# A hybrid decoder trunk: gate and up with seven block products for eight in two k pairs of eight, and each FFN in two parts

## The chip, the core and the metric

The kernel runs on one core of one Trainium2 chip. The metric is the device time of one execution in microseconds; the median over several runs counts. Engines are named as in the profile: PE is TensorE's matmul, PEld its weight load, DVE is VectorE, ACT is ScalarE, POOL is GpSimd, SP is the queue that issues the weight transfers.

## The reference, cut to what matters

Two layers work on a residual stream of 256 tokens by 2048 channels in float32. Each layer is a mixer with its output projection, and then a SwiGLU FFN with a hidden width of 5632:

```
h = h + mix(rms_norm(h, norm_mix[layer]))
h = h + swiglu(rms_norm(h, norm_ffn[layer]), w_gate[layer], w_up[layer], w_down[layer])

def swiglu(xn, w_gate, w_up, w_down):
    return (jax.nn.silu(xn @ w_gate) * (xn @ w_up)) @ w_down
```

The mixer of layer 0 is sliding-window attention beside an mLSTM, that of layer 1 is forgetting attention; a final rms_norm follows. The change touches the FFNs, and the output projections only in that they also prepare operands for it.

## The kernel before, in words

Tokens are two tiles of 128 (`NT` = 2, index t), the channels 16 k tiles of 128 (`KT`), and output columns come in blocks of 512 (`NB`), which is one PSUM bank per token tile.

Every float32 product is made of three float32r matmuls. An operand is split into a rounded high part and the rest: x is hi + lo, and the product is hi*hi + hi*lo + lo*hi (lines 158 to 160 of `gemm`). The activations are split once: `xh`, `xl` hold the normalised stream, transposed, and `mh`, `ml` hold the input of the next projection. Weights are streamed: `load_raw` brings a chunk of two k tiles by 512 columns (512 KB) through SP into one of four `raw` buffers, `load_chunk` has ScalarE copy it to `hi` (line 135) and VectorE subtract to get `lo` (line 136); `hi` and `lo` have four buffers each. A chunk feeds 12 matmuls: two k tiles, two token tiles, three products.

PSUM has eight banks: pool `pa` with four for accumulators, pool `pm` with four for transposes and the like.

`ffn` runs over 11 groups g of 512 hidden columns. In a group, `project` computes gate over the 16 k tiles (8 chunks, 96 matmuls), ScalarE applies Silu with the row scale r (line 328), `project` computes up (another 96 matmuls), VectorE multiplies (line 331), TensorE transposes the result in eight 128x128 blocks (line 339, tile `pf`), and `split_plain` writes it, split, to `mh`, `ml` (the first 16 k tiles) or to `eh`, `el` (the other 28). After all 11 groups, w_down is applied in four column blocks over 44 k tiles each, and `add_out` (line 216) adds to the residual `h`, or `finish` in layer 1.

`out_proj` before it does two column blocks at a time; behind each block it adds to `h`, transposes `h` (`split_scaled`: tiles `pt`, `xh`, `xl`, lines 199 to 206) and sums squares (line 181). Tiles are allocated in rings, and an instruction waits by semaphore for what it reads and for the buffer that it writes. The order of the instructions within each engine's queue is decided at build time by the scheduler of the tile framework, from the program's order and its own estimates; on the chip each queue runs in that order.

Of the kernel before, what the change touches and what calls it, by code (L numbers as in the profile page):

```python
# [7 lines left out]
F32 = mybir.dt.float32  # L8
F32R = mybir.dt.float32r
AF = mybir.ActivationFunctionType  # L10
ALU = mybir.AluOpType
# [4 lines left out]
P = 128  # L16
D = 2048
S = 256
NT = S // P
KT = D // P  # L20
FF = 5632
NB = 512
CK = 2
# [7 lines left out]
OFF_QM, OFF_KM, OFF_VM, OFF_OM = 1536, 2048, 2560, 3584  # L31
CAP = 15.0
FILL = 24


@with_exitstack
def trunk(
# [20 lines left out]
    nc = tc.nc  # L58
# [6 lines left out]
    wp = ctx.enter_context(tc.tile_pool(name="wp", bufs=4))  # L65
# [5 lines left out]
    pa = ctx.enter_context(tc.tile_pool(name="pa", bufs=4, space=PSUM))  # L71
    pm = ctx.enter_context(tc.tile_pool(name="pm", bufs=4, space=PSUM))
# [20 lines left out]
    for n in range(4):  # L93
# [27 lines left out]
    gT = cp.tile([P, 4 * KT], F32, name="gT")  # L121
# [8 lines left out]

    def load_chunk(w, k0, c0, n):
        raw = ahead.pop(0) if ahead else load_raw(w, k0, c0, n)
        hi = wp.tile([P, CK, NB], F32R, tag="hi", name="hi")
        lo = wp.tile([P, CK, NB], F32R, tag="lo", name="lo")
        nc.scalar.copy(hi[:, :, 0:n], raw[:, :, 0:n])  # L135
        nc.vector.tensor_tensor(  # L136
            out=lo[:, :, 0:n], in0=raw[:, :, 0:n], in1=hi[:, :, 0:n].bitcast(F32), op=ALU.subtract
        )
        return hi, lo
# [4 lines left out]
    def gemm(acc, lhs, w, c0, n, k_from, k_to, k_all, skew=1):  # L144
        k0 = k_from
        while k0 < k_to:
            last = k_to == k_all and k0 + skew * CK >= k_all
            chunks = [load_chunk(w, kc, c0, n) for kc in range(k0, k_all if last else k0 + CK, CK)]
            order = [(i, t) for i in range(len(chunks) * CK) for t in range(NT)]
            if last:  # L150
                order.sort(key=lambda it: it[1])
            for i, t in order:
                k = k0 + i
                hi, lo = (c[:, i % CK, 0:n] for c in chunks[i // CK])
                ah, al = lhs(k)
                ts = slice(t * P, (t + 1) * P)
                o = acc[t][:, 0:n]
                nc.tensor.matmul(o, ah[:, ts], hi, start=(k == 0), stop=False)  # L158
                nc.tensor.matmul(o, ah[:, ts], lo, start=False, stop=False)  # L159
                nc.tensor.matmul(o, al[:, ts], hi, start=False, stop=(k == k_all - 1))  # L160
# [32 lines left out]
    def split_scaled(idx, n):  # L193
        for half in range(2):
            pt = pm.tile([P, 2, NT, P], F32, tag="pm", name="pt")
            for i in range(2):
                k = 4 * n + 2 * half + i
                for t in range(NT):
                    nc.tensor.transpose(pt[:, i, t, :], h[:, t, k * P : (k + 1) * P], ident)  # L199
            for i in range(2):  # L200
                k = 4 * n + 2 * half + i
                src = pt[:, i, :, :].rearrange("p t q -> p (t q)")
                g = gT[:, idx * KT + k : idx * KT + k + 1]
                nc.scalar.mul(xh[:, k, :], src, g)  # L204
                nc.vector.scalar_tensor_tensor(
                    out=xl[:, k, :], in0=src, scalar=g, in1=xh[:, k, :].bitcast(F32), op0=ALU.mult, op1=ALU.subtract
                )

    def split_plain(dst_h, dst_l, src):
        nc.scalar.copy(dst_h, src)  # L210
        nc.vector.tensor_tensor(out=dst_l, in0=src, in1=dst_h.bitcast(F32), op=ALU.subtract)

    def add_out(acc, n):
        for t in range(NT):
            o = h[:, t, n * NB : (n + 1) * NB]
            nc.vector.tensor_tensor(out=o, in0=acc[t], in1=o, op=ALU.add)
# [85 lines left out]
    def out_proj(w, idx, key):  # L302
        last = KT - 4
        for n0 in (0, 2):
            accs = [new_acc() for _ in range(2)]
            for i in range(2):
                gemm(accs[i], m_of, w, (n0 + i) * NB, NB, 0, last, KT)
            for i in range(2):
                gemm(accs[i], m_of, w, (n0 + i) * NB, NB, last, KT, KT)
                add_out(accs[i], n0 + i)  # L310
                split_scaled(idx, n0 + i)
                square_sum(key, n0 + i)

    def ffn(layer, key, idx_next=None, key_next=None, finish=None):
        with tc.tile_pool(name=f"fp{layer}", bufs=2) as fp:
            rest = FF // P - KT
            eh = fp.tile([P, rest, S], F32R, name="eh", bufs=1)
            el = fp.tile([P, rest, S], F32R, name="el", bufs=1)

            def a_of(k):  # L320
                return m_of(k) if k < KT else (eh[:, k - KT, :], el[:, k - KT, :])

            r = rstd(key)
            for g in range(FF // NB):
                ga = project(w_gate[layer], g * NB, NB)
                sg = fp.tile([P, NT, NB], F32, tag="sg", name="sg")
                for t in range(NT):
                    nc.scalar.activation(sg[:, t, :], ga[t], AF.Silu, scale=r[:, t : t + 1])  # L328
                ua = project(w_up[layer], g * NB, NB)
                for t in range(NT):  # L330
                    nc.vector.scalar_tensor_tensor(
                        out=sg[:, t, :], in0=ua[t], scalar=r[:, t : t + 1], in1=sg[:, t, :], op0=ALU.mult, op1=ALU.mult
                    )
                for half in range(2):
                    pt = pm.tile([P, 2, S], F32, tag="pm", name="pf")
                    for i in range(2):
                        c = (2 * half + i) * P
                        for t in range(NT):
                            nc.tensor.transpose(pt[:, i, t * P : (t + 1) * P], sg[:, t, c : c + P], ident)  # L339
                    k = 4 * g + 2 * half  # L340
                    if k < KT:
                        split_plain(mh[:, k : k + 2, :], ml[:, k : k + 2, :], pt)
                    else:
                        split_plain(eh[:, k - KT : k - KT + 2, :], el[:, k - KT : k - KT + 2, :], pt)
            for n in range(4):
                acc = new_acc()
                end = idx_next is None and n == 3
                gemm(acc, a_of, w_down[layer], n * NB, NB, 0, FF // P, FF // P, skew=3 if end else 1)
                if idx_next is None:
# [14 lines left out]
    r = rstd("m0")  # L364
# [413 lines left out]
```

## Time and profile before

| what | value |
|---|---|
| median of 3 runs | 2213.86 us (2213.74 to 2215.78) |
| the profiled execution's own time | 2215.41 us |
| its span, first to last instruction | 2213.7 us |
| mean granted TensorE clock | 0.998 |
| HBM read | 404.48 MB, 184 GB/s over the span |
| one weight chunk (512 KB), issue to landing | 3.5 us median |

In a line of a group, the part before the first bar names line, engine, operation, tiles and shapes and count; then come the busy time in us and the mean of one in ns; then the idle time just before them on their engine and what ended it. In the timeline a row has start, duration (us), engine, line, operation, count, and in brackets the idle time before it. In the table by stretches each engine has its busy time and the count of instructions, followed by the granted clock, the share of the DMA engines and GB/s. PE rows overlap, since matmuls are pipelined.

### The profile page before, as it was taken

The page shows a single profiled execution, that of the slowest core. Times are in us where ns is not written, and L with a number is a line of the kernel's source. Part 1 is how long each engine was busy: PE and PEld are TensorE (multiplying, and loading weights), DVE is VectorE, ACT ScalarE, POOL GpSimd, SP SyncE. Part 2 cuts the span into 40 slices and gives each one's busy share as a digit, 9 for nine tenths or more (in the row PEclk, how much of TensorE's full clock was granted, in tenths as well). Part 3 has the DMA queues.
Part 4 walks back from the last instruction along what each step waited for, and adds up shares of the span by engine and source line. Part 5 has one row for each costly group of instructions (what it writes and reads, how often), then busy time and mean ns, then how long its engine had stood idle before and what let it go on. Part 6 is the DMA issues. An engine that isn't in the chain of part 4 may idle for free.

```text
span 2213.7 us, 26201 instructions
## 1 busy us (share of the span) xinstructions
PE 2194.0 (99%) x10184; PEld 1821.8 (82%) x10184; DVE 1148.7 (52%) x1256; ACT 1003.1 (45%) x1275; POOL 39.4 (2%) x61
## 2 busy tenths in 40 slices
PE   8999999999999999999999999999999999999998
PEld 6878888888888888888888888888888888888886
DVE  5565555454445444444555555654454445544543
ACT  5564445444444443444445444544444444444443
POOL 2110000000000000000010000000000000000000
PEclk9999999999999999999999999999999999999999
DMA  7444555656665665555675555556665666555664
GB/s 258 144 153 151 163 171 190 191 185 192 190 190 185 190 190 190 190 190 191 182 228 165 168 171 166 177 185 191 190 190 186 190 190 190 189 190 191 195 194 142
DMA packets 213532, 408.30 MB, mean 184 GB/s; under 512 B 12736, under 2 KB 21024, under 8 KB 213152
## 3 DMA queue, kind: packets, MB, share of 16 engines
q1 hardware_dynamic: 212736, 402.90, 57.7%
q0 software_dynamic: 624, 3.72, 0.5%
q8 instruction: 79, 1.29, 0.2%
q14 instruction: 45, 0.37, 0.0%
q10 hardware_dynamic: 48, 0.02, 0.0%
HBM read 404.48 MB, written 2.11 MB: 184 GB/s over the span
## 4 chain that ended last, share of the span: by engine, by line
PE 98%; ACT 1%; DMA 1%; issue 0%; DVE 0%; SPq 0%; DVEq 0%; POOLq 0%; POOL 0%; ACTq 0%
PE acc L159 31%; PE acc L158 31%; PE acc L160 31%; PE pf L339 1%; DMA h<-in_x_dram 1%; PE p L239 1%; PE ptm L222 1%; PE pt L199 1%; PE po L290 1%; PE pp L282 0%; ACT s L261 0%; PE p L232 0%; PE po L291 0%; ACT hi L135 0%; PE pp L286 0%
## 5 line engine op out<-in xcount | busy, mean ns | idle before, releaser
L136 DVE TENSOR_TENSOR lo<-raw,hi 128x1024 fp32r<-128x1024 f32 (+2 forms) x776 | 935.1, 1207 | 939.3 <-ACT hi L135 935.0
L135 ACT CAST hi<-raw 128x1024 fp32r<-128x1024 f32 (+2 forms) x776 | 802.7, 1036 | 1047.6 <-PE acc L160 1014.6
L159 PE MATMUL acc<-lo,xh 128*128 128x512 f32 (+3 forms) x2144 | 826.1, 385 | 0.4 <-DVE lo L136 0.4
L158 PE MATMUL acc<-hi,xh 128*128 128x512 f32 (+3 forms) x2144 | 825.1, 386 | 1.2 <-ACT hi L135 1.2
L160 PE MATMUL acc<-hi,xl 128*128 128x512 f32 (+3 forms) x2144 | 824.2, 385 | 0.0
L158 PEld LDWEIGHTS acc<-hi,xh 128*128 128x128 f32 x2144 | 402.6, 188 | 81.1 <-issue 2.0
L159 PEld LDWEIGHTS acc<-lo,xh 128*128 128x128 f32 x2144 | 403.4, 188 | 79.0 <-DVE lo L136 1.1
L160 PEld LDWEIGHTS acc<-hi,xl 128*128 128x128 f32 x2144 | 403.3, 188 | 78.0 <-issue 0.3
L158 PE MATMUL acc<-hi,mh 128*128 128x512 f32 x512 | 200.8, 392 | 1.2 <-ACT mh L210 1.2
L159 PE MATMUL acc<-lo,mh 128*128 128x512 f32 x512 | 200.9, 393 | 0.0
L160 PE MATMUL acc<-hi,ml 128*128 128x512 f32 x512 | 198.7, 390 | 0.0
L158 PE MATMUL acc<-hi,eh 128*128 128x512 f32 x448 | 174.1, 389 | 0.0
L159 PE MATMUL acc<-lo,eh 128*128 128x512 f32 x448 | 174.1, 389 | 0.0
L160 PE MATMUL acc<-hi,el 128*128 128x512 f32 x448 | 174.1, 389 | 0.0
L158 PEld LDWEIGHTS acc<-hi,mh 128*128 128x128 f32 x512 | 96.1, 188 | 21.1 <-ACT mh L210 1.4
L160 PEld LDWEIGHTS acc<-hi,ml 128*128 128x128 f32 x512 | 96.2, 188 | 19.6
L159 PEld LDWEIGHTS acc<-lo,mh 128*128 128x128 f32 x512 | 96.1, 188 | 19.6
L158 PEld LDWEIGHTS acc<-hi,eh 128*128 128x128 f32 x448 | 84.1, 188 | 17.5
L159 PEld LDWEIGHTS acc<-lo,eh 128*128 128x128 f32 x448 | 84.1, 188 | 17.5
L160 PEld LDWEIGHTS acc<-hi,el 128*128 128x128 f32 x448 | 84.1, 188 | 17.3
L328 ACT ACTIVATE sg<-acc,r 128x512 f32<-128x512 f32 x44 | 30.2, 690 | 19.5 <-PE acc L160 19.5
L204 ACT ACTIVATE xh<-pt,gT 128x256 fp32r<-128x256 f32 x64 | 27.8, 470 | 18.0 <-PE pt L199 16.3
(222 smaller groups left out, 717.9 us busy)
## 6 DMA issues: line engine op xcount, KB each, us to landing
raw<-in_w_gate_dram SPq DMA_DIRECT2D x176, 512.0 KB, 3.5
raw<-in_w_up_dram SPq DMA_DIRECT2D x176, 512.0 KB, 3.5
raw<-in_w_down_dram SPq DMA_DIRECT2D x176, 512.0 KB, 3.6
raw<-in_w_in_odd_dram SPq DMA_DIRECT2D x88, 512.0 KB, 3.8
raw<-in_w_in_even_dram SPq DMA_DIRECT2D x64, 512.0 KB, 3.7
raw<-in_w_out_even_dram SPq DMA_DIRECT2D x32, 512.0 KB, 3.6
raw<-in_w_out_odd_dram SPq DMA_DIRECT2D x32, 512.0 KB, 3.7
raw<-in_w_in_odd_dram SPq DMA_DIRECT2D x8, 272.0 KB, 2.8
```

The costliest lines, as they stand in the source:

```text
L135: nc.scalar.copy(hi[:, :, 0:n], raw[:, :, 0:n])
L136: nc.vector.tensor_tensor(out=lo[:, :, 0:n], in0=raw[:, :, 0:n], in1=hi[:, :, 0:n].bitcast(F32), op=ALU.subtract)
L158: nc.tensor.matmul(o, ah[:, ts], hi, start=(k == 0), stop=False)
L159: nc.tensor.matmul(o, ah[:, ts], lo, start=False, stop=False)
L160: nc.tensor.matmul(o, al[:, ts], hi, start=False, stop=(k == k_all - 1))
L199: nc.tensor.transpose(pt[:, i, t, :], h[:, t, k * P : (k + 1) * P], ident)
L204: nc.scalar.mul(xh[:, k, :], src, g)
L222: nc.tensor.transpose(pt[:, i, :], s_, ident)
L239: nc.tensor.matmul(p1[:, jj, :], q_of(j, 1), k_of(j), start=True, stop=True)
L290: nc.tensor.matmul(po, v_of(j, 0), t0[:, j, :], start=True, stop=False)
L328: nc.scalar.activation(sg[:, t, :], ga[t], AF.Silu, scale=r[:, t : t + 1])
L339: nc.tensor.transpose(pt[:, i, t * P : (t + 1) * P], sg[:, t, c : c + P], ident)
```

## The change

Gate and up of one pair of k tiles (a, b) for the two token tiles (0, 1) are a 2x2 block product: [x0a x0b; x1a x1b] times [ga ua; gb ub], with blocks of 128x128 against 128x512. It takes eight block products. For the pairs 2 and 3 (`MIXED`) out of eight, the new `gate_up` uses the form with seven products, in which sums and differences of blocks are multiplied. The sums on the side of the activations (`sh`, `sl`, four per pair) are made once a layer by `sums_of`, called from `split_scaled` in `out_proj`. The differences on the side of the weights (`t4`, lines 378 to 381 of the changed file) are made for each group and pair by VectorE, and split into `ht`, `lt`; only half of the up chunk is still split by itself (`hu`, `lu`). Three of the seven products add directly into one of the accumulators `plain`; four go into banks of their own (`mixed`, tiles `prod`), which serve both pairs and are combined at the end of the group by VectorE and added to `plain` (lines 405 to 413), into tile `c`.

Since four `plain` and four `mixed` banks are held at once, gate and up of a group run together over the k pairs, in the order of `ORDER`, and the two PSUM pools change roles from group to group (`bank`, `par`). Silu, the product, the transposes and the split follow as before (lines 428 to 443).

Each FFN is done in two parts of 6 and 5 groups (`HALVES`): after each part w_down is applied to that part's k tiles (24 and 20), with an `add_out` each. `eh`, `el` shrink from 28 k tiles to 8. The pool of the FFN is opened before `out_proj` by the new `close_layer`.

The diff, cut (in `split_scaled` and `out_proj` the argument `extra` is passed through; `split_chunk` is the second half of the old `load_chunk`):

```diff
+ORDER = ((0, 0), (0, 1), (1, 2), (0, 4), (0, 5), (1, 3), (0, 6), (0, 7))
+MIXED = [p for w, p in ORDER if w]
+HALVES = (0, 6, 11)
...
+    def sums_of(extra, pair, src):
+        sh, sl, pool = extra
+        full = pool.tile([P, 2, NT, P], F32, tag="tmp", name="full")
+        for i in range(2):
+            g = src[1][i]
+            nc.scalar.mul(full[:, i, :, :].rearrange("p t q -> p (t q)"), src[0][i], g)
+        s = pool.tile([P, 4, P], F32, tag="tmp", name="s4")
+        nc.vector.tensor_tensor(out=s[:, 0, :], in0=full[:, 0, 1, :], in1=full[:, 1, 1, :], op=ALU.add)
+        nc.vector.tensor_tensor(out=s[:, 1, :], in0=s[:, 0, :], in1=full[:, 0, 0, :], op=ALU.subtract)
+        nc.vector.tensor_tensor(out=s[:, 2, :], in0=full[:, 0, 0, :], in1=full[:, 0, 1, :], op=ALU.subtract)
+        nc.vector.tensor_tensor(out=s[:, 3, :], in0=full[:, 1, 0, :], in1=s[:, 1, :], op=ALU.subtract)
+        j = MIXED.index(pair)
+        split_plain(sh[:, j, :, :], sl[:, j, :, :], s)
...
+    def three(o, ah, al, hi, lo, start, stop):
+        nc.tensor.matmul(o, ah, hi, start=start, stop=False)
+        nc.tensor.matmul(o, ah, lo, start=False, stop=False)
+        nc.tensor.matmul(o, al, hi, start=False, stop=stop)
+
+    def bank(par, name):
+        return pm.tile([P, NB], F32, tag="pm", name=name) if par else pa.tile([P, NB], F32, tag="acc", name=name)

+    def gate_up(fp, sh, sl, layer, g, par):
+        c0 = g * NB
+        plain = [[bank(par, "acc") for _ in range(NT)] for _ in range(2)]
+        mixed = None
+        count = [s_[0] for s_ in ORDER]
+        for pos, (w, pair) in enumerate(ORDER):
+            k0 = 2 * pair
+            if not w:
+                for m, wt in enumerate((w_gate[layer], w_up[layer])):
+                    hi, lo = load_chunk(wt, k0, c0, NB)
+                    for i in range(CK):
+                        ah, al = x_of(k0 + i)
+                        for t in range(NT):
+                            ts = slice(t * P, (t + 1) * P)
+                            three(
+                                plain[m][t], ah[:, ts], al[:, ts], hi[:, i, :], lo[:, i, :],
+                                pos == 0 and i == 0, pos == len(ORDER) - 1 and i == CK - 1,
+                            )
+                continue
+            first, last = 1 not in count[:pos], 1 not in count[pos + 1 :]
+            if first:
+                mixed = [bank(1 - par, "prod") for _ in range(4)]
+            rg = load_raw(w_gate[layer], k0, c0, NB)
+            ru = load_raw(w_up[layer], k0, c0, NB)
+            hg, lg = split_chunk(rg, NB)
+            t4 = fp.tile([P, 4, NB], F32, tag="t4", name="t4", bufs=1)
+            nc.vector.tensor_tensor(out=t4[:, 0, :], in0=ru[:, 0, :], in1=rg[:, 0, :], op=ALU.subtract)
+            nc.vector.tensor_tensor(out=t4[:, 1, :], in0=ru[:, 1, :], in1=ru[:, 0, :], op=ALU.subtract)
+            nc.vector.tensor_tensor(out=t4[:, 2, :], in0=ru[:, 1, :], in1=t4[:, 0, :], op=ALU.subtract)
+            nc.vector.tensor_tensor(out=t4[:, 3, :], in0=rg[:, 1, :], in1=t4[:, 2, :], op=ALU.subtract)
+            hu = wp.tile([P, CK, NB], F32R, tag="hi", name="hi")
+            lu = wp.tile([P, CK, NB], F32R, tag="lo", name="lo")
+            split_plain(hu[:, 1, :], lu[:, 1, :], ru[:, 1, :])
+            ht, lt = [], []
+            for i in range(2):
+                hs = fp.tile([P, 2, NB], F32R, tag="ht", name="ht")
+                ls = fp.tile([P, 2, NB], F32R, tag="lt", name="lt")
+                split_plain(hs, ls, t4[:, 2 * i : 2 * i + 2, :])
+                ht += [hs[:, 0, :], hs[:, 1, :]]
+                lt += [ls[:, 0, :], ls[:, 1, :]]
+            j = MIXED.index(pair)
+            xa, la = x_of(k0)
+            xb, lb = x_of(k0 + 1)
+            t0, t1 = slice(0, P), slice(P, 2 * P)
+            three(mixed[0], xa[:, t0], la[:, t0], hg[:, 0, :], lg[:, 0, :], first, last)
+            three(plain[0][0], xb[:, t0], lb[:, t0], hg[:, 1, :], lg[:, 1, :], False, False)
+            three(plain[1][0], sh[:, j, 3, :], sl[:, j, 3, :], hu[:, 1, :], lu[:, 1, :], False, False)
+            three(mixed[1], sh[:, j, 0, :], sl[:, j, 0, :], ht[0], lt[0], first, last)
+            three(mixed[2], sh[:, j, 2, :], sl[:, j, 2, :], ht[1], lt[1], first, last)
+            three(mixed[3], sh[:, j, 1, :], sl[:, j, 1, :], ht[2], lt[2], first, last)
+            three(plain[0][1], xb[:, t1], lb[:, t1], ht[3], lt[3], False, False)
+        c = fp.tile([P, 4, NB], F32, tag="c", name="c", bufs=1)
+        u2 = fp.tile([P, NB], F32, tag="tmp", name="u2")
+        nc.scalar.copy(c[:, 0, :], mixed[0])
+        nc.vector.tensor_tensor(out=u2, in0=mixed[3], in1=c[:, 0, :], op=ALU.add)
+        nc.vector.tensor_tensor(out=c[:, 1, :], in0=mixed[2], in1=u2, op=ALU.add)
+        nc.vector.tensor_tensor(out=c[:, 2, :], in0=mixed[1], in1=u2, op=ALU.add)
+        nc.vector.tensor_tensor(out=c[:, 3, :], in0=mixed[1], in1=c[:, 1, :], op=ALU.add)
+        for m in range(2):
+            for t in range(NT):
+                o = c[:, 2 * m + t, :]
+                nc.vector.tensor_tensor(out=o, in0=plain[m][t], in1=o, op=ALU.add)
+        return c

-            r = rstd(key)
-            for g in range(FF // NB):
-                ga = project(w_gate[layer], g * NB, NB)
-                sg = fp.tile([P, NT, NB], F32, tag="sg", name="sg")
...
-                ua = project(w_up[layer], g * NB, NB)
...
-            for n in range(4):
-                acc = new_acc()
...
-                gemm(acc, a_of, w_down[layer], n * NB, NB, 0, FF // P, FF // P, skew=3 if end else 1)
+        r = rstd(key)
+        for part in range(2):
+            g0, g1 = HALVES[part : part + 2]
+            nk = 4 * (g1 - g0)
+            for g in range(g0, g1):
+                par = (g - g0 + part) % 2
+                c = gate_up(fp, sh, sl, layer, g, par)
+                for t in range(NT):
+                    nc.scalar.activation(c[:, t, :], c[:, t, :], AF.Silu, scale=r[:, t : t + 1])
+                for t in range(NT):
+                    nc.vector.scalar_tensor_tensor(
+                        out=c[:, t, :], in0=c[:, 2 + t, :], scalar=r[:, t : t + 1], in1=c[:, t, :], op0=ALU.mult, op1=ALU.mult
+                    )
...
+            wd = w_down[layer][4 * g0 * P : 4 * g1 * P, :]
+            for n in range(4):
+                acc = new_acc()
+                end = part == 1 and idx_next is None and n == 3
+                gemm(acc, a_of, wd, n * NB, NB, 0, nk, nk, skew=3 if end else 1)
+                if part == 0:
+                    add_out(acc, n)
+                elif idx_next is None:
+                    finish(acc, n)
+                else:
+                    add_out(acc, n)
+                    split_scaled(idx_next, n)
+                    square_sum(key_next, n)
...
+    def close_layer(layer, w_out, idx, key, **rest):
+        with tc.tile_pool(name=f"fp{layer}", bufs=2) as fp:
+            deep = max(4 * (b - a) for a, b in zip(HALVES, HALVES[1:])) - KT
+            eh = fp.tile([P, deep, S], F32R, name="eh", bufs=1)
+            el = fp.tile([P, deep, S], F32R, name="el", bufs=1)
+            sh = fp.tile([P, len(MIXED), 4, P], F32R, name="sh", bufs=1)
+            sl = fp.tile([P, len(MIXED), 4, P], F32R, name="sl", bufs=1)
+            out_proj(w_out, idx, key, (sh, sl, fp))
+            ffn(layer, fp, sh, sl, eh, el, key, **rest)
...
-    out_proj(w_out_even[0], 2, "f0")
-    ffn(0, "f0", 1, "m1")
+    close_layer(0, w_out_even[0], 2, "f0", idx_next=1, key_next="m1")
...
-    out_proj(w_out_odd[0], 3, "f1")
...
-    ffn(1, "f1", finish=finish)
+    close_layer(1, w_out_odd[0], 3, "f1", finish=finish)
```

More of the change, by code (lines that the diff above doesn't have):

```diff
@@ L132, in load_chunk, with split_chunk @@
         raw = ahead.pop(0) if ahead else load_raw(w, k0, c0, n)
+        return split_chunk(raw, n)
+    def split_chunk(raw, n):
         hi = wp.tile([P, CK, NB], F32R, tag="hi", name="hi")
@@ L206, in split_scaled @@
                     out=xl[:, k, :], in0=src, scalar=g, in1=xh[:, k, :].bitcast(F32), op0=ALU.mult, op1=ALU.subtract
+                )
+            if extra is not None and 2 * n + half in MIXED:
+                k = 4 * n + 2 * half
+                sums_of(
+                    extra,
+                    2 * n + half,
+                    (
+                        [pt[:, i, :, :].rearrange("p t q -> p (t q)") for i in range(2)],
+                        [gT[:, idx * KT + k + i : idx * KT + k + i + 1] for i in range(2)],
+                    ),
                 )
@@ L300, in attention, with out_proj @@
             split_plain(mh[:, ks, :], ml[:, ks, :], po)
-    def out_proj(w, idx, key):
+    def out_proj(w, idx, key, extra):
         last = KT - 4
@@ L310, in out_proj @@
                 add_out(accs[i], n0 + i)
-                split_scaled(idx, n0 + i)
+                split_scaled(idx, n0 + i, extra)
                 square_sum(key, n0 + i)
[L314 to L321, printed above, removed]
-            r = rstd(key)
-            for g in range(FF // NB):
-                ga = project(w_gate[layer], g * NB, NB)
-                sg = fp.tile([P, NT, NB], F32, tag="sg", name="sg")
+    def three(o, ah, al, hi, lo, start, stop):
+        nc.tensor.matmul(o, ah, hi, start=start, stop=False)
+        nc.tensor.matmul(o, ah, lo, start=False, stop=False)
+        nc.tensor.matmul(o, al, hi, start=False, stop=stop)
@@ L327, in ffn, with a_of @@
+    def ffn(layer, fp, sh, sl, eh, el, key, idx_next=None, key_next=None, finish=None):
+        def a_of(k):
+            return m_of(k) if k < KT else (eh[:, k - KT, :], el[:, k - KT, :])
+        r = rstd(key)
[5 more added lines that the diff above has]
+                c = gate_up(fp, sh, sl, layer, g, par)
                 for t in range(NT):
-                    nc.scalar.activation(sg[:, t, :], ga[t], AF.Silu, scale=r[:, t : t + 1])
@@ L334, in ffn @@
                 for half in range(2):
-                    pt = pm.tile([P, 2, S], F32, tag="pm", name="pf")
+                    pt = bank(par, "pf").rearrange("p (i q) -> p i q", i=2)
                     for i in range(2):
-                        c = (2 * half + i) * P
+                        cs = (2 * half + i) * P
                         for t in range(NT):
-                            nc.tensor.transpose(pt[:, i, t * P : (t + 1) * P], sg[:, t, c : c + P], ident)
-                    k = 4 * g + 2 * half
+                            nc.tensor.transpose(pt[:, i, t * P : (t + 1) * P], c[:, t, cs : cs + P], ident)
```

6 lines of the change are left out of this document (2 added, 4 removed).

## The prediction

> **What bounds the kernel now.** I read the page's busy times first, then its chain, then busy times by stretch, then the timeline of TensorE and of VectorE inside one FFN group.
>
> ```profile
> PE 2194.0 (99%) x10184; PEld 1821.8 (82%) x10184; DVE 1148.7 (52%) x1256; ACT 1003.1 (45%) x1275; POOL 39.4 (2%) x61
> ...
> PE 98%; ACT 1%; DMA 1%; issue 0%; DVE 0%; SPq 0%; DVEq 0%; POOLq 0%; POOL 0%; ACTq 0%
> ```
>
> TensorE is busy all the time and is also 98% of the chain that ended last, so nothing else sets the end. The question is what one matmul costs and whether anything becomes later than TensorE once matmuls are taken away. Two stretches of one FFN group each; the groups' transposes stand 44.4 to 44.5 us apart from 403 to 848 us, so the others look the same:
>
> ```profile
> core 0: us, PE busy (x) PEld busy (x) DVE busy (x) ACT busy (x) POOL busy (x), PEclk, DMA share, GB/s
> 670.06:714.51 44.45, 44.45 (x203) 36.84 (x201) 22.21 (x20) 19.11 (x20) 0.00 (x0) 1.00 0.61 189
> 714.51:758.95 44.44, 44.44 (x203) 36.84 (x201) 22.21 (x20) 19.11 (x20) 0.00 (x0) 1.00 0.61 190
> ```
>
> A group takes 44.45 us, with TensorE never idle, VectorE at 50%, ScalarE at 43%, DMA at 61% and the granted clock at 1.00. The timeline gives the price of a matmul:
>
> ```profile
> 699.61 0.39 PE L158 MATMUL acc<-hi,xh 128*128 128x512 f32 x1
> 699.84 0.39 PE L159 MATMUL acc<-lo,xh 128*128 128x512 f32 x1
> 700.07 0.39 PE L160 MATMUL acc<-hi,xl 128*128 128x512 f32 x1
> 700.29 0.39 PE L158 MATMUL acc<-hi,xh 128*128 128x512 f32 x1
> ```
>
> The rows' duration is 0.39 us, but the starts are 0.2267 us apart (0.68 per three): matmuls overlap, and one that goes away is worth the distance, not the duration. Check: 192 matmuls x 0.2267 = 43.5, and the eight transposes cost 0.89 (between 713.90 and 715.24 stand eight of them and two matmuls: 1.34 - 0.45); together 44.4, the group.
>
> **The change, part by part. TensorE.** A pair of k tiles (gate and up, two row blocks) took 8 block products x 3 matmuls = 24; by `three` it takes 7 x 3 = 21. Two pairs in eight: 6 matmuls fewer in a group, 6 x 22 groups = 132 of 10184, and the built programs differ on this engine by exactly 132. Transposes and w_down's matmuls stay as many. 132 x 0.2267 = 29.9 us removed; a group becomes 43.1 us. The matmuls that read `sh`, `sl`, `ht`, `lt` are not in the trace; `acc<-hi,eh` and `acc<-hi,mh` in w_down have the same 0.227 between starts with other tiles on both sides, so I bound theirs by the same number from both sides. A mixed pair carries up to eight waits on matmuls instead of four; in the groups above 64 waits leave 0.04 us over, so met waits are free (0.2 us in all at most).
>
> The rule in the Trainium skill, TensorE: Matmul & The Clock Gate, section Back-to-back issue gap, gives N/2.4 + 2.5 = 216 ns for 512 columns; by it the saving would be an estimated 28.5 us. The trace has 226.7 ns, 5% longer, and the trace decides.
>
> **VectorE, the sum.** These rows price it:
>
> ```profile
> L136 DVE TENSOR_TENSOR lo<-raw,hi 128x1024 fp32r<-128x1024 f32 x744 | 911.8, 1227 | 920.6 <-ACT hi L135 916.6
> L331 DVE SCALAR_TENSOR_TENSOR sg<-acc,r,sg 128x512 f32<-128x512 f32 x44 | 30.9, 743 | 0.0
> L216 DVE TENSOR_TENSOR h<-acc,h 128x512 f32<-128x512 f32 x24 | 15.9, 684 | 2.9 <-PE acc L160 2.9
> L136 DVE TENSOR_TENSOR lo<-raw,hi 128x512 fp32r<-128x512 f32 x16 | 12.0, 747 | 10.5 <-ACT hi L135 10.2
> L717 DVE TENSOR_TENSOR h<-h,gf 128x512 f32<-128x512 f32 x6 | 3.9, 683 | 0.0
> ```
>
> Before, a group is 16 `lo` x 1.227 + 2 x 0.743 + 2 `ml` x 0.686 = 22.5 us (the stretches say 22.2, 20 instructions). After: 12 plain `lo` 14.7; each mixed pair has one `lo` 1.227, four `t4` differences of SBUF tiles (L717 and the 128x512 `lo` bound them at 0.683 and 0.747; 0.69 taken, the row with the same output type), `lu` 0.747 and two `lt` 2 x 1.227, so 7.2, twice 14.4; the eight combining adds of L406 to L413 read PSUM like L216, 5.5; gating 1.5; `ml` 1.4. Sum 37.4 us in 40 instructions, against 43.1 us of TensorE: 87%, close, but below. ScalarE: 14 x 1.05 for chunks, 4 x 1.05 for `ht`, 2 x 0.62 for `hu`, and copy, Silu and `mh` 3.2, so 23.3 of 43.1.
>
> Is it the sum, or less? Where nothing is waited for, VectorE starts the next instruction before the last ends:
>
> ```profile
> 707.70 1.22 DVE L136 TENSOR_TENSOR lo<-raw,hi 128x1024 fp32r<-128x1024 f32 x1 [1.49 <-ACT hi L135]
> 708.84 1.40 DVE L331 SCALAR_TENSOR_TENSOR sg<-acc,r,sg 128x512 f32<-128x512 f32 x2
> 710.43 1.23 DVE L136 TENSOR_TENSOR lo<-raw,hi 128x1024 fp32r<-128x1024 f32 x1 [0.18 <-ACT hi L135]
> ```
>
> 708.84 is 0.08 ahead of the end at 708.92. I keep full durations as the careful side; 40 x 0.08 = 3.2 us less is the other bound. The skill speaks against the change here: VectorE: DVE Perf Modes, section The DRAIN you can't avoid, has the next instruction wait until the pipe is empty, which would leave the full 37.4; this trace shows the overlap instead.
>
> **VectorE, the order.** A sum below 100% can still be late at one place, so I laid out one group in the built order. Time 0 is the group's first matmul; chunks A to D (two plain pairs) take 2.72 us each, so C ends at 8.4 with the two transposes inside it, the first mixed matmul (hi only) comes at 8.8, its `lo` at 12.2, `lu` at 13.4, the last `lt` at 14.7, the following chunk's `lo` at 15.6, and at 16.5 the third product, whose bank the transposes held until `ml`. VectorE behind it: the hi and lo rings are four deep, so `lo` of chunk B may run at -4.2, when the chunk four places earlier is done. From there it is nearly solid: B's `lo` to -2.9, two adds to -1.6, C's `lo` to -0.2, an add to 0.5, two `t4` to 2.0 (the second raw tile lands 3.5 us after the `lo` that frees it, at 0.6), the last add 2.7, gating 3.4, `t4` 4.1, D's `lo` 5.3, gating 6.1, `lt` 7.3, `t4` 8.0, mixed `lo` 9.2, `lu` 9.9, `lt` 11.2, next `lo` 12.4, two `ml` 13.8. Against the needs (12.2, 13.4, 14.7, 15.6, 16.5) the margins are 3.0, 3.5, 3.5, 3.2 and 2.7 us. The transposes need gating by 7.5 and 10.0: margins over 3.9. The second mixed pair has no combining in front of it: its last tile is ready about 25, wanted from 27.4 on. Mixed products are read out (`u2` and three adds, done 7.7 us before the next group) long before the bank is wanted again. So each stall is costed at nothing, covered by 2.7 us; beyond that it costs its excess in each of 22 groups.
>
> **The rest.** `sums_of` adds, twice a layer, about 1.5 us of ScalarE and 1.8 of VectorE (four 128x128 by the row L274 at 0.281, one split) under out_proj's matmuls, where chunks use 1.05 and 1.23 of 2.72. Two parts add 16 adds of 0.684 under w_down, where VectorE is busy 125.8 of 255 us. The passage from a part's last group to w_down, of which there are now two a layer, has 27 matmuls (6.1 us) in front of the first transposes, and gating is done 2.7 after the group's end, since no `t4` stands in between: free, with 3.4 us to spare. Where out_proj hands to the first group, VectorE has the adds to h, eight `xl` and the first mixed pair together; by the same layout the smallest margin is 2 us. I put 0 to 3 us on it, 0.4 taken (it lies nearer to zero by that margin), twice. The number of weight loads from HBM is unchanged. POOL and SP get no new work on this path: SP issues the same transfers, in gate-up order, each behind a raw tile freed at least 3.5 us before use.
>
> **Sum.** Profiled execution: 2215.4 (span 2213.7) - 29.9 + 0.8 = 2186.3. The median of the runs is 1.55 below that execution: 2184.8.
>
> **Rivals.** (a) VectorE gets late at the first mixed pair. Against: margins of 2.7 us and more with full durations. For: 15 instructions stand in that row, and if each paid the 0.18 hand-over seen at 710.43, the 2.7 is gone; with `t4` and adds at 0.747 another 0.5 us falls on TensorE, 22 x 0.5 = 11: 2196. (b) VectorE becomes the bound, the other sign: all 40 pay 0.18 (7.2 us) and the sixteen new two-input operations cost 0.747 (1.0 us), 37.4 + 8.2 = 45.6 us a group against 44.45 before; 22 x 1.15 = 25 us: 2239. It decides from 7.0 us of waiting in a group on. Against: before, VectorE's instructions that have work queued show no such gap. (c) The passages stall: both hand-overs from out_proj and both new ones to w_down at 3 us each: 2196. (d) The saving is the row duration, 132 x 0.39 = 51 us, 2163; the spacing in the timeline speaks against it. That the products are not fewer is excluded by the count.
>
> **Numbers.** Forecast 80%; (a) and (c) together 11%; (b) 7%; (d) 2%. The range runs from 132 x 0.2267 with nothing lost and 1.5 us of scatter (2182) to (a) and (c), 2197. Within 0.2% (4.4 us) a measurement can't tell from no change: 2% lies there, between (a) and (b); faster 91%, slower 7%.
>
> **What would show it.** In the changed profile: 132 fewer TensorE instructions; a group of 43.1 us; TensorE at 99%; VectorE about 37 us a group. Wrong would be TensorE waits on L241's or L142's tiles of more than a few us in all, or a group above 43.5.

## The result and the profile after

The changed kernel takes 2186.98 us (median of 4 runs, 2185.16 to 2187.78), the kernel before 2214.82 in the runs beside it (4 runs, 2213.74 to 2217.05). The ratio is 0.9872, 95% interval 0.9855 to 0.9889: faster by 1.28%. The profiled execution took 2186.29 us with a span of 2184.6, so 29.1 us less of span than before. The prediction had 2184.8 (2182 to 2197).

The busy line and the chain of the page, after:

```profile
PE 2164.8 (99%) x10052; PEld 1796.9 (82%) x10052; DVE 1442.0 (66%) x1732; ACT 1078.5 (49%) x1397; POOL 38.4 (2%) x61
...
PE 98%; ACT 1%; DMA 1%; issue 0%; DVE 0%; SPq 0%; POOLq 0%; POOL 0%; ACTq 0%
```

TensorE has 132 instructions fewer and is still 98% of the chain that ended last; VectorE took on 293 us of work and holds 0% of it. Two groups, cut at their transposes:

```profile
core 0: us, PE busy (x) PEld busy (x) DVE busy (x) ACT busy (x) POOL busy (x), PEclk, DMA share, GB/s
449.83:492.96 43.13, 43.13 (x196) 35.69 (x195) 34.80 (x41) 22.25 (x25) 0.00 (x0) 1.00 0.64 195
492.96:536.08 43.12, 43.12 (x196) 35.68 (x195) 34.59 (x41) 22.17 (x25) 0.00 (x0) 1.00 0.62 195
```

A group went from 44.45 to 43.125 us, 1.325 less, and 22 x 1.325 = 29.15 is the whole difference of the spans: everything was gained inside the groups, and nothing was lost between them. TensorE's waits all lie before the first FFN group (the last at 301.7 us), and the kernel before has the same; none is for a tile of the block products. The three longest:

```profile
PE pg L128 <- DMA gn<-in_norm_mix_dram: 3.9, 1, 3.9
PE pt L219 <- DMA h<-in_x_dram: 3.8, 2, 2.4
PE acc L164 <- ACT hi L141: 1.2, 2, 0.7
```

VectorE's new rows among the costliest groups of instructions (L413 reads PSUM, L378 and `lo` and `lt` at L241 read SBUF):

```profile
L413 DVE TENSOR_TENSOR c<-acc,c 128x512 f32<-128x512 f32 x88 | 57.9, 683 | 0.0
L378 DVE TENSOR_TENSOR t<-raw 128x512 f32<-128x512 f32 x44 | 30.5, 693 | 46.2 <-DMA raw<-in_w_up_dram 27.2 <-issue 19.0
L241 DVE TENSOR_TENSOR lo<-raw,hi 128x512 fp32r<-128x512 f32 x44 | 30.1, 684 | 0.0
L241 DVE TENSOR_TENSOR lt<-t,ht 128x1024 fp32r<-128x1024 f32 x88 | 107.2, 1218 | 0.0
```

And VectorE's timeline in the group whose first matmul starts at 483.01, around its first mixed pair:

```profile
483.90 0.69 DVE L378 TENSOR_TENSOR t<-raw 128x512 f32<-128x512 f32 x1 [0.50 <-DMA raw<-in_w_up_dram]
...
490.51 1.22 DVE L142 TENSOR_TENSOR lo<-raw,hi 128x1024 fp32r<-128x1024 f32 x1
491.64 0.69 DVE L241 TENSOR_TENSOR lo<-raw,hi 128x512 fp32r<-128x512 f32 x1
492.25 1.22 DVE L241 TENSOR_TENSOR lt<-t,ht 128x1024 fp32r<-128x1024 f32 x1
493.38 1.22 DVE L142 TENSOR_TENSOR lo<-raw,hi 128x1024 fp32r<-128x1024 f32 x1
494.52 1.28 DVE L241 TENSOR_TENSOR ml<-pf,mh 128x512 fp32r<-128x512 f32 x2
```

TensorE's timeline in the same group shows when each of these tiles is first read, the last row being the third product, whose bank `ml` frees:

```profile
495.30 0.40 PE L346 MATMUL prod<-lo,xh 128*128 128x512 f32 x1
496.44 0.39 PE L346 MATMUL acc<-lo,sh 128*128 128x512 f32 x1
497.80 0.39 PE L346 MATMUL acc<-lt,xh 128*128 128x512 f32 x1
498.71 0.39 PE L346 MATMUL acc<-lo,xh 128*128 128x512 f32 x1
499.62 0.39 PE L345 MATMUL prod<-ht,sh 128*128 128x512 f32 x1
```

Counted from 483.01, the five tiles are ready at 8.7, 9.3, 10.5, 11.6 and 12.8 and are read at 12.3, 13.4, 14.8, 15.7 and 16.6: margins of 3.6, 4.1, 4.3, 4.1 and 3.8 us, where the prediction laid out 3.0, 3.5, 3.5, 3.2 and 2.7.

### The profile page after: what moved, and what is told of

It reads as the page before. It is cut to its first block, busy times and chain, and to the rows that moved or that the text cites. A ratio compares the mean times of both kernels' runs of the same rounds, so it can differ in the third digit from the quotient of the medians.

```text
span 2184.6 us, 26574 instructions
## 1 busy us (share of the span) xinstructions
PE 2164.8 (99%) x10052; PEld 1796.9 (82%) x10052; DVE 1442.0 (66%) x1732; ACT 1078.5 (49%) x1397; POOL 38.4 (2%) x61
## 3 DMA queue, kind: packets, MB, share of 16 engines
q8 instruction: 78, 1.28, 0.2%
## 4 chain that ended last, share of the span: by engine, by line
PE 98%; ACT 1%; DMA 1%; issue 0%; DVE 0%; SPq 0%; POOLq 0%; POOL 0%; ACTq 0%
PE acc L164 17%; PE acc L165 17%; PE acc L166 17%; PE acc L346 12%; PE acc L347 12%; PE acc L345 12%; PE prod L346 2%; PE prod L345 2%; PE prod L347 2%; PE pf L438 1%; DMA h<-in_x_dram 1%; PE p L269 1%; PE ptm L252 1%; PE pt L219 1%; PE po L320 1%; PE pp L312 0%
## 5 line engine op out<-in xcount | busy, mean ns | idle before, releaser
L142 DVE TENSOR_TENSOR lo<-raw,hi 128x1024 fp32r<-128x1024 f32 (+3 forms) x732 | 876.7, 1206 | 597.0 <-ACT hi L141 595.7
L141 ACT CAST hi<-raw 128x1024 fp32r<-128x1024 f32 (+3 forms) x732 | 752.3, 1034 | 825.3 <-PE acc L166 515.1
L347 PE MATMUL acc<-hi,xl 128*128 128x512 f32 x1100 | 429.7, 391 | 0.0
L346 PE MATMUL acc<-lo,xh 128*128 128x512 f32 x1100 | 428.5, 390 | 0.0
L345 PE MATMUL acc<-hi,xh 128*128 128x512 f32 x1100 | 423.8, 391 | 0.0
L164 PE MATMUL acc<-hi,mh 128*128 128x512 f32 x768 | 300.6, 392 | 1.2 <-ACT mh L240 1.2
L165 PE MATMUL acc<-lo,xh 128*128 128x512 f32 (+3 forms) x736 | 276.3, 376 | 0.4 <-DVE lo L142 0.4
L164 PE MATMUL acc<-hi,xh 128*128 128x512 f32 (+3 forms) x736 | 275.2, 378 | 1.2 <-ACT hi L141 1.2
L166 PE MATMUL acc<-hi,xl 128*128 128x512 f32 (+3 forms) x736 | 276.2, 376 | 0.0
L241 DVE TENSOR_TENSOR lt<-t,ht 128x1024 fp32r<-128x1024 f32 x88 | 107.2, 1218 | 0.0
```

Of the source, the lines that this page charges most:

```text
L142: nc.vector.tensor_tensor(out=lo[:, :, 0:n], in0=raw[:, :, 0:n], in1=hi[:, :, 0:n].bitcast(F32), op=ALU.subtract)
L345: nc.tensor.matmul(o, ah, hi, start=start, stop=False)
L346: nc.tensor.matmul(o, ah, lo, start=False, stop=False)
L347: nc.tensor.matmul(o, al, hi, start=False, stop=stop)
```

## The experiments

The theory to be tested: the time falls by the distance of TensorE's starts for each matmul that goes away, as long as VectorE's tiles come before TensorE reads them; running gate and up together, and the two parts, cost nothing. The rivals: a share of the gain or of a hidden loss belongs to the joint order or to the parts; and, where more is asked of VectorE, either its sum in a group or the place of its work in its queue decides.

**Taking the products out, and doing one pair.** `e1_no_products` keeps the joint order, the two parts and the roles of the pools, and does all eight pairs with eight block products; `e2_one_pair` has one mixed pair.

```diff
-ORDER = ((0, 0), (0, 1), (1, 2), (0, 4), (0, 5), (1, 3), (0, 6), (0, 7))
+ORDER = tuple((0, p) for p in range(8))
...
-        nc.scalar.copy(c[:, 0, :], mixed[0])
-        nc.vector.tensor_tensor(out=u2, in0=mixed[3], in1=c[:, 0, :], op=ALU.add)
...
-        return c
+        return plain, c
```

The eight adds and `sums_of` go with it, and Silu and gating read the accumulators. The other one:

```diff
-ORDER = ((0, 0), (0, 1), (1, 2), (0, 4), (0, 5), (1, 3), (0, 6), (0, 7))
+ORDER = ((0, 0), (0, 1), (1, 2), (0, 3), (0, 4), (0, 5), (0, 6), (0, 7))
```

> All eight pairs plain: 192 matmuls a group as before, but gate and up together, pools swapped from group to group, FFN in two parts; no sh, t4, ht, no combining adds. Theory (the saving is the 132 matmuls x 0.2267 us, the rest costs nothing): a group of 44.45 us, time within 0.1% of the kernel before (2213 to 2217 us). Rival (the two parts and the joint order cost or bring something by themselves, hidden in the result): off by over 3 us, for example 2205 if the joint order had removed passages, 2220 if the new passages to w_down stall.

> Only pair 2 by seven products: 66 matmuls fewer than before. Theory: half of the way, 66 x 0.2267 = 15.0 us less than before, group 43.8 us, about 2200. Rival (a matmul is worth its row's 0.39 us and the changed kernel lost the other 20 us in stalls at the second pair): 2189 or lower. Rival (the combining tail costs a fixed amount per group): less than 14 us gained.

Without the products 2215.53 us against 2215.65 before, ratio 1.0000 (0.9991 to 1.0010), with the span of the kernel before, 2213.7. So the joint order and the two parts neither give nor cost anything that this interval of 0.1% (2 us) would show, and the gain is that of the products. With one pair 2201.05, 14.6 us less than before, ratio 0.9933 (0.9918 to 0.9948); 66 matmuls x 0.2267 = 15.0. Zero, one and two pairs stand at 0, 14.6 and 28 us: linear in the count.

**Loading VectorE.** `m4_both` is the change with idle work: each mixed pair's `t4` (128x2048) goes through two more passes on VectorE that leave it as it is.

```diff
+            for _ in range(2):
+                nc.vector.tensor_tensor(out=t4, in0=t4, in1=t4, op=ALU.max)
```

> The change with two idle passes over t4 more in each mixed pair (max of t4 with itself, 128x2048, about 2.2 us each, the values stay): 8.8 us more on VectorE a group, 43.6 against 43.1 on TensorE. Theory of the prediction's rival (VectorE is the bound as soon as its sum passes TensorE's): 44 to 46 us a group, 2207 to 2250. Rival (only the place counts, and the scheduler moves the products behind the delay): 2187 to 2195.

2225.61 us, ratio 1.0044 (1.0028 to 1.0060): slower than before. A stretch of 45 us, and TensorE's first two waits in the whole run:

```profile
449.00:494.00 45.00, 43.87 (x194) 35.09 (x193) 42.84 (x44) 22.14 (x26) 0.00 (x0) 1.00 0.59 185
```
```profile
PE prod L345 <- ACT hi L141: 12.3, 18, 0.7
PE prod L345 <- ACT ht L240: 7.5, 16, 0.6
```

A group takes 43.125 + (2224.9 - 2184.6) / 22 = 44.96 us. The four passes (2.29 us each by their row) bring VectorE to 42.8 us a group, which is still below the 43.1 that TensorE needs, and yet the group is 1.8 us longer. The waits stand under ScalarE. The chain of the run between 460 and 464 shows what they are:

```profile
460.65 0.24 PE acc L347
460.91 1.05 ACT hi L141
461.96 0.96 ACT ht L240
...
462.96 0.74 PE prod L345 x2
```

This `hi` belongs to the second mixed pair. By the profile it was released by a matmul that had just ended, in this and in all the other 17 waits of its kind; the `ht` of the first mixed pair stands behind it in ScalarE's queue, and TensorE waits for both. VectorE is not in this piece of the chain and holds 4% of the whole. So the time fell into the range that the rival gave, but not by its mechanism: VectorE is not the bound here. That the scheduler built a worse order round the idle work is likely, and was not tested.

**More pairs.** `e3_three_pairs` mixes three pairs; by the count it should gain another 15 us.

```diff
-ORDER = ((0, 0), (0, 1), (1, 2), (0, 4), (0, 5), (1, 3), (0, 6), (0, 7))
+ORDER = ((0, 0), (0, 1), (1, 2), (0, 5), (1, 3), (0, 6), (1, 4), (0, 7))
```

> Pairs 2, 3, 4 by seven products, in the order 0 1 (2) 5 (3) 6 (4) 7: 198 matmuls fewer than before, 66 fewer than the change. Theory (TensorE's count decides while VectorE's sum stays below it): TensorE 183 x 0.2267 + 0.96 = 42.4 us a group, VectorE 34.8 + 3.9 = 38.7, so 22 x 0.68 = 15 us below the change: 2172. Rival (VectorE late at one place, since three pairs stand close together): 1 us lost a group, 2194.

2188.77 us, ratio 0.9885 (0.9869 to 0.9902): no better than two pairs, 17 us off what was expected. The chain of the page and one stretch:

```profile
PE 76%; DVE 11%; DMA 8%; ACT 2%; issue 2%; SPq 0%; DVEq 0%; ACTq 0%; POOLq 0%; POOL 0%
```
```profile
494.60:538.00 43.40, 42.24 (x188) 34.02 (x188) 37.38 (x45) 21.64 (x25) 0.00 (x0) 1.00 0.59 194
```

VectorE stands in the chain with DMA in front of it, although in the stretch it is only 86% busy: it is late without being full. Its timeline at the end of a group tells why:

```profile
525.04 1.22 DVE L142 TENSOR_TENSOR lo<-raw,hi 128x1024 fp32r<-128x1024 f32 x1
529.28 0.69 DVE L378 TENSOR_TENSOR t<-raw 128x512 f32<-128x512 f32 x1 [3.02 <-DMA raw<-in_w_up_dram]
529.89 0.69 DVE L379 TENSOR_TENSOR t<-raw 128x512 f32<-128x512 f32 x1
530.49 0.68 DVE L407 TENSOR_TENSOR c<-prod,u 128x512 f32<-128x512 f32 x1
```

VectorE works its queue in order. The next group's first `t4` was placed ahead of the combining adds; its up chunk had not landed, and the adds, ready since the products ended, lay 3.02 us behind it. The work put off reached TensorE at 534.16, which waited 0.82 us for a `lo`:

```profile
534.16 0.50 PE L346 MATMUL acc<-lo,xh 128*128 128x512 f32 x1 [0.82 <-DVE lo L142]
```

A later kernel separates the sum from the place. `e9_three_late` has the same three mixed pairs, so the same work for VectorE, with the first of them one pair later:

```diff
-ORDER = ((0, 0), (0, 1), (1, 2), (0, 5), (1, 3), (0, 6), (1, 4), (0, 7))
+ORDER = ((0, 0), (0, 1), (0, 5), (1, 2), (0, 6), (1, 3), (1, 4), (0, 7))
```

> Three pairs in two parts, as in e3, in the order 0 1 5 (2) 6 (3) (4) 7: the first mixed pair has one more plain pair in front of it. Theory (in e3 VectorE is late at the first pair, because the combining of the group before is in front of it): most of the 17 us lost comes back, 2172 to 2182. Rival (VectorE at 38.7 of 42.4 us is late wherever the pairs stand): 2187 to 2195, the wait now at the last pair or at the transposes.

2172.83 us (2171.60 to 2174.47), ratio 0.9808 (0.9793 to 0.9822): the fastest of all, 14 us below the change. The chain and one stretch:

```profile
PE 93%; DVE 2%; DMA 2%; ACT 1%; issue 1%; SPq 0%; DVEq 0%; POOLq 0%; POOL 0%; ACTq 0%
```
```profile
495.51:537.93 42.42, 42.42 (x193) 35.13 (x192) 38.44 (x47) 23.88 (x27) 0.00 (x0) 1.00 0.64 199
```

And VectorE's timeline at the end of the same group:

```profile
523.41 0.69 DVE L406 TENSOR_TENSOR u<-prod,c 128x512 f32<-128x512 f32 x1 [0.71 <-PE prod L347]
524.14 0.69 DVE L407 TENSOR_TENSOR c<-prod,u 128x512 f32<-128x512 f32 x1
...
532.40 0.74 DVE L430 SCALAR_TENSOR_TENSOR c<-c,r 128x512 f32<-128x512 f32 x1
533.06 0.68 DVE L378 TENSOR_TENSOR t<-raw 128x512 f32<-128x512 f32 x1
```

VectorE is at 91%, more than in `e3_three_pairs`, and TensorE never waits in the group, which takes the 42.42 us that the count gives (43.125 less three spacings). The adds now run through, and `t4` follows the gating, when its chunk has long landed. So not the sum stalled `e3_three_pairs`, but the place of the work. That it was the one waiting instruction is what the timeline says; the other order also gives the first mixed pair's tiles one plain pair (5.4 us) more time, and what share of the 16 us belongs to which was not split.

`e4_four_pairs` goes one further, in three parts of 5, 5 and 1 groups (with as many parts in the loop over parts):

```diff
-ORDER = ((0, 0), (0, 1), (1, 2), (0, 4), (0, 5), (1, 3), (0, 6), (0, 7))
-HALVES = (0, 6, 11)
+ORDER = ((0, 0), (0, 1), (1, 2), (1, 3), (0, 6), (1, 4), (1, 5), (0, 7))
+HALVES = (0, 5, 10, 11)
```

> Pairs 2 to 5 by seven products, and the FFN in three parts (5, 5, 1 groups) so that the tiles fit: 264 matmuls fewer than before. Theory (the sum on VectorE becomes the bound): VectorE 34.8 + 2 x 3.9 = 42.6 us a group against 41.8 on TensorE, with its unavoidable waits 43 to 45 us a group, so nothing more is gained than with two pairs: 2183 to 2225. Rival (only TensorE's count matters): 264 x 0.2267 = 59.8 us below before, 2156.

2274.84 us, ratio 1.0265 (1.0250 to 1.0280): outside what either theory gave. One group, and TensorE's waits:

```profile
457.34:503.93 46.59, 43.97 (x189) 33.95 (x188) 42.75 (x53) 25.68 (x29) 0.00 (x0) 1.00 0.56 181
```
```profile
PE pf L438 <- DVE c L430: 27.6, 4, 8.1
PE acc L345 <- ACT hi L141: 23.7, 33, 2.4
PE prod L345 <- ACT ht L240: 13.8, 30, 0.5
```

VectorE's 42.75 us a group are above the 41.8 that TensorE would need (43.125 less six spacings), so here the sum alone forbids the 41.8; but the group takes 46.6, more than either, and the first wait, 27.6 us, lies at four passages to w_down and came with the three parts. Two things were changed at once, and this run alone doesn't price them.

**Handing work to GpSimd.** `e5_three_pool` gives one of the four differences of `e3_three_pairs` to GpSimd.

```diff
-            nc.vector.tensor_tensor(out=t4[:, 1, :], in0=ru[:, 1, :], in1=ru[:, 0, :], op=ALU.subtract)
+            nc.gpsimd.tensor_tensor(out=t4[:, 1, :], in0=ru[:, 1, :], in1=ru[:, 0, :], op=ALU.subtract)
```

> Three pairs as before, but the difference ru1 - ru0 of each mixed pair is made by GpSimd (about 2.5 us each by the row of 128x256 at 1.28 us) and no longer by VectorE (0.6 us each). Theory (three pairs lose because VectorE is late, at 88% of a group): 1.8 us less on VectorE a group, most of the 17 us loss goes, 2172 to 2178. Rival (GpSimd's difference is itself late, or holds up VectorE's two-input instructions while it runs): 2187 or more.

2227.76 us, ratio 1.0061 (1.0038 to 1.0084), 39 us worse than without it. In the profiled execution, which took 2235.84 us, the longest of the four, VectorE has 66 instructions of 0.69 us less and is yet busier, 1543.0 us against 1524.8. Its timeline, with GpSimd's:

```profile
489.79 1.78 POOL L379 TENSOR_TENSOR t<-raw 128x512 f32<-128x512 f32 x1 [16.79 <-DMA raw<-in_w_up_dram]
490.33 2.31 DVE L142 TENSOR_TENSOR lo<-raw,hi 128x1024 fp32r<-128x1024 f32 x1
```

A `lo` that takes 1.23 elsewhere takes 2.31 beside GpSimd's subtraction, which itself takes 1.79 on average where VectorE's took 0.69. What share of the 39 us is this hold-up, and what the later `t4`, wasn't split. The Trainium skill, SBUF — State Buffer, section Who interferes with whom, says that a VectorE instruction with two inputs in SBUF contends with a GpSimd instruction that reads SBUF; these rows agree.

**The passages.** `e6_three_own` splits a mixed pair's chunks into buffers of their own, so that they don't turn the rings of four that plain chunks use (three mixed pairs in the order of `e3_three_pairs`), and makes room for that by parts of 4, 4 and 3 groups, which need no `eh`, `el`. `e7_three_own_pool` is the same with GpSimd's difference.

```diff
-HALVES = (0, 6, 11)
+HALVES = (0, 4, 8, 11)
...
-            hg, lg = split_chunk(rg, NB)
+            hg = fp.tile([P, CK, NB], F32R, tag="hgm", name="hg", bufs=1)
+            lg = fp.tile([P, CK, NB], F32R, tag="lgm", name="lg", bufs=1)
+            split_plain(hg, lg, rg)
...
+            hu = fp.tile([P, NB], F32R, tag="hum", name="hu", bufs=2)
+            lu = fp.tile([P, NB], F32R, tag="lum", name="lu", bufs=2)
+            split_plain(hu, lu, ru[:, 1, :])
```

> Three pairs, the split of a mixed pair's gate chunk and half up chunk in buffers of their own in the pool of the FFN and not in the hi and lo rings, so that VectorE may prepare them earlier and the plain chunks keep all four ring places; for the room, the FFN in three parts (4, 4, 3 groups). The same instructions on VectorE apart from 16 more adds to h. Theory (it is lateness at a place, not the sum): 2172 to 2180. Rival (VectorE's sum of 38.7 in 42.4 us leaves no room whatever the buffers): 2187 to 2192.

> Both at once: three pairs, own buffers, three parts, ru1 - ru0 on GpSimd. Theory: 42.4 us a group, all of the 198 x 0.2267 = 44.9 us less than before, 2171. Rival as for the two alone: no better than the better of them.

2223.37 us, ratio 1.0032 (1.0022 to 1.0042), and 2258.38, ratio 1.0199 (1.0179 to 1.0218): both far from the 2171 to 2180 that the theory gave. TensorE in `e6_three_own` at a passage from a part's last group to w_down:

```profile
785.83 0.39 PE L347 MATMUL acc<-hi,xl 128*128 128x512 f32 x1
791.39 0.69 PE L440 MATMUL pf<-ident,c 128*128 128x128 f32 x2 [5.17 <-DVE c L432]
791.73 0.77 PE L164 MATMUL acc<-hi,mh 128*128 128x512 f32 x1
```

In place of 27 matmuls of w_down ahead of the transposes there are none, and TensorE waits four times, 20.7 us in all. w_down's accumulators come from the pool `pa`. `par` of a part's last group says where that group's plain accumulators lie: with parts of 6 and 5 always in the other pool, with parts of 4, 4 and 3 (and of 5, 5 and 1) in `pa` itself at two passages of each layer, so that w_down can't begin until they are read. To test that, `e8_three_own_par` turns the roles so that every part ends as in the change, and nothing else; `e10_par_flip` turns them the wrong way in the change itself.

The first against `e6_three_own`, the second against the change:

```diff
-                par = (g - g0 + part) % 2
+                par = (g1 - g) % 2
```
```diff
-                par = (g - g0 + part) % 2
+                par = (g - g0 + part + 1) % 2
```

> Own buffers and three parts as in e6, but the pools are dealt so that the last group of every part has its plain accumulators in pm, and w_down's accumulators (pa) don't wait for that group's adds. In e6 four passages cost 5.2 us of wait and a spell of half clock (6.83 us, worth 3.4) each, 35 us in all. Theory: these go, 2223 - 35 = 2188 or a little less. Rival (the passages are late for another reason): 2215 or more.

> The change with the roles of the two PSUM pools swapped in every group, nothing else: the last group of each part now has its plain accumulators in pa, where w_down's go. Theory (the passage to w_down is free in the change because w_down's first matmuls stand in front of the transposes): in the swapped form the transposes come first and wait for VectorE, about 5 us of wait and 3 us of half clock at each of four passages, 2187 + 32 = 2219. Rival (the scheduler finds other work for TensorE there): within 5 us of the change.

`e8_three_own_par` takes 2189.21 us, ratio 0.9884 (0.9869 to 0.9899), 34 us less than `e6_three_own`, as expected, and no wait for `pf` is left. It isn't better than `e3_three_pairs` either: buffers of their own, with the third part, brought nothing. `e10_par_flip` takes 2209.93, ratio 0.9973 (0.9962 to 0.9984), 23 us above the change, less than expected. Its waits:

```profile
PE acc L345 <- DVE tot L193: 6.9, 2, 3.5
PE pf L438 <- DVE c L430: 6.2, 4, 1.5
...
PE pt L219 <- DVE h L246: 3.6, 2, 1.8
```

Four passages to w_down cost 1.5 us each here, and no matmul of w_down stands in front of the transposes at any of them; more (10.5 us) fell at the two hand-overs from out_proj, whose first group then takes its plain accumulators from `pm`, which the transposes just before it use too. Together 16.7 us of the 24.3 by which the spans differ. More than half of the remaining 7.6 is the clock behind those waits. One stretch of 7 us right after a hand-over in `e10_par_flip`, and the same stretch in the change:

```profile
362.00:369.00 7.00, 7.00 (x25) 5.54 (x24) 2.76 (x7) 1.78 (x3) 0.69 (x1) 0.75 0.06 19
```
```profile
362.00:369.00 7.00, 7.00 (x33) 5.79 (x32) 6.23 (x10) 4.34 (x6) 0.69 (x1) 1.00 0.72 218
```

TensorE is busy in both and does 25 matmuls instead of 33, about 1.8 us lost; behind the other hand-over the granted clock is 0.51 over 5.7 us, which is about 2.8 us. Why a passage costs 1.5 us here and 5.2 in `e6_three_own` was not taken apart; there the last mixed pair stands one pair nearer to the end of the group, so that its adds have 5.4 us less to be done in.

## Why the prediction was right, step by step

**TensorE, 132 x 0.2267 = 29.9.** Right: the spans differ by 29.1, and one pair alone gave 14.6 of 15.0. Rival (d), the row's duration of 0.39, would have given 51 and is excluded. The missing 0.8 us is spread over the groups: 43.125 measured against 44.45 - 6 x 0.2267 = 43.09. Which matmuls hold these 0.035 us a group wasn't traced. The 216 ns that the prediction takes from the Trainium skill, TensorE: Matmul & The Clock Gate, section Back-to-back issue gap, stand there for an isolated matmul; for a stream of weight loads and matmuls the section has about 131 ns, and this trace has neither.

**VectorE, 37.4 us a group in 40 instructions.** Measured 34.6 and 34.8 in the two stretches, near the lower bound (34.2). The rows were taken well (combining adds 0.683 against 0.684, `t4` 0.684 to 0.693 against 0.69, `lt` 1.218 against 1.227); only `lu` was too dear, at 0.747 against 0.684. What made the sum too large was to keep full durations: the 0.08 us overlap, seen at one place before, holds in the other rows too (1.22 rows start 1.13 to 1.14 apart above). The section of the Trainium skill that the prediction names for it, VectorE: DVE Perf Modes, The DRAIN you can't avoid, goes on to say that a next instruction that is not held starts earlier, so it does not speak against these rows.

**VectorE's order.** The layout held to within 1.0 us, and every margin was larger than laid out. Its one late item, the `t4` behind the raw tile, began at 0.9 instead of 0.6; the up chunk lands 4.5 us after its issue here (median), where 3.5 was taken. The same row is the one that stood in front of the adds in `e3_three_pairs`.

**The passages, free, and 0.8 at the hand-overs.** Free was right, and the 0.8 was not spent there; that the sum of 2186.3 meets the profiled 2186.29 to the hundredth is luck, as the 0.8 stands for the wrong place. The reason given, 27 matmuls in front, holds only by the roles of the pools, which the prediction did not name: with them turned, `e10_par_flip` loses 23 us of the 28, 6.2 of them as waits at these passages and 10.5 at the hand-overs. Rival (c) had a real mechanism, close by.

**The median 1.55 below the profiled execution.** That step missed: after, the median is 0.7 above it, which is why the point was 2.2 us low. It was scatter of three runs: the median of before was 2214.8 to 2215.7 in the later sets, and the ratio applied to the first one, 2213.86 x 0.9872, gives 2185.5.

**Rivals (a) and (b).** Neither came; no tile of the first mixed pair was late. The point from which (b) decides, 7.0 us more in a group, rested on a sum that was 2.7 too large: it would be 9.7 on the measured one. `m4_both` added 9.2 and already lost to the kernel before, with VectorE's sum still below TensorE's and VectorE at 4% of the chain: the order failed before the sum was full. Whether VectorE becomes the bound in the way that (b) says stays open.

## What to carry to other kernels

Price a removed matmul by the distance of starts in a full stream, and the work that replaces it by the engine's own starts; then lay out the queue of the engine that takes it over, and look there for an instruction that waits for a DMA ahead of ready work: three mixed pairs lost 16 us in one order, with VectorE at 86%, and nothing within a group in another, at 91%. Where a loop alternates buffers between two pools, look at which pool the last turn before the next stage leaves occupied: one parity was worth 23 to 34 us here. Compare the length of a group with its count of starts, not only the list of waits.

## What the runs showed of the hardware

- A wait costs more than the idle time that the profile shows for it (matmul ends are modelled there). Around the 5.17 us wait above, the starts lie 5.56 us apart where 0.2267 is usual: 5.33 lost, 0.16 more than the idle, because the last row (0.39) outlasts its spacing. A delay below 0.16 us therefore shows no idle at all in these rows. In `e3_three_pairs` TensorE's idle is 10.1 us above that of `e9_three_late` (2187.2 - 2157.6 against 2171.0 - 2151.5), while the spans differ by 16.2; the other 6.1 is in "busy" time.
- Waits of 2.45 us (`e5_three_pool`) and 5.17 us (`e6_three_own`) were followed by starts 0.43 us apart for 3.2 and 4.7 us; so was a wait of 3.48 us with another of 1.79 shortly before (`e10_par_flip`, 4 us). The Trainium skill, TensorE: Matmul & The Clock Gate, section HAM oscillation, puts the limit at gaps of over about 3.4 us. A gap of 2.45 us was enough for it here, and so were gaps of 2.08, 2.10 and 2.21 us in the same run; a gap of 2.39 us in `e4_four_pairs` left the granted clock at 1.00. So the length of one gap alone does not decide it, and what else does was not traced. Behind the gap of 2.45 us, and behind that of 2.39:

```profile
566.12:569.32 3.20, 3.20 (x8) 2.53 (x9) 3.20 (x5) 0.27 (x1) 0.00 (x0) 0.50 0.58 164
2054.40:2060.00 5.60, 5.14 (x21) 3.93 (x22) 3.77 (x6) 2.00 (x2) 0.00 (x0) 1.00 0.66 227
```

- GpSimd's 128x512 subtraction takes 1.79 us against VectorE's 0.69, and held a VectorE instruction up for 1.08 us; the kernel with 66 of them took 39 us longer.
